# An encoder block with pooling and mLSTM branches: the pooling mixer folded into the input weights, gating and weight splitting moved, row mathematics transposed on TensorE

## The chip, the cores and the metric

The kernel runs on one core of a Trainium2 chip. The metric is the device time in microseconds of one execution, as a median over runs. TensorE (PE in the profile) multiplies matrices, VectorE (DVE), ScalarE (ACT) and GpSimd (POOL) do the rest, and SyncE (SP) issues all DMA transfers from one queue, in order.

## What is computed

The input x is 2048 tokens by 1024 channels in float32. It is normalised and multiplied with one wide matrix, whose columns give u and z (pooling branch), q, k, v, o, z_b and 16 gate columns (mLSTM branch), and the merge gates g_a and g_b.

```python
h = rms_norm(x, norm_pre_g)
u_a, z_a, q, k, v, o, z_b, gates, g_a, g_b = split(h @ w_in)
pooled = multiscale_pool(u_a)              # per group of 256 channels: window mean (2, 4, 8, 16) minus the token
mixed = einsum('bsgc,gcd->bsgd', pooled, pool_mix_w)
y_a = mixed * pool_scale * silu(z_a)
# q, k: depthwise convolution of width 5 and silu; four heads of 256
# two directions of a gated matrix memory in chunks of 128 tokens, with a running maximum over the chunks
y_b = normalised(h_fwd + h_bwd) * sigmoid(o) * silu(z_b)
merged = sigmoid(g_a + b0) * (y_a @ w_proj_pool) + sigmoid(g_b + b1) * (y_b @ w_proj_mlstm)
out = x + rms_norm(merged @ w_out, norm_post_g)
```

Pooling is linear and acts along the tokens, the same for all channels of a group; the mixer is linear and acts along the channels.

## The kernel before

Products are made to about float32 accuracy: each operand is split into a high and a low part (`split`, lines 92 to 99: ScalarE copies the high part, VectorE or GpSimd subtracts the low one), and three matmuls are made for each pair (`mm3`, lines 107 to 109; `acc3`, lines 932 to 934). A few products use plain float32 operands in one matmul, which the profile records as two.

**Phase 1** goes twice over 1024 tokens (a half). `operands` loads the transposed x in two blocks of 512 columns, scales it with the rows `rb` of inverse norms, and makes the eight operand blocks A11 to S4. In the first half `sums(b)` squares each block on ScalarE, adds the squares on VectorE, and adds over the partitions with matmuls into `ssqp` (line 249). Then 36 pairs of 128 columns follow in an order that `in_pairs` writes out; each after the first two is a product of seven blocks by a Strassen-like scheme (`strassen`), 84 matmuls of 512 columns, in PSUM banks A, B and C. The weights of a pair stand in the pool `wc` (20 rooms, 14 to a pair, a high and a low part in each two). In the first half `prep_w` makes them and `keep_w` stores four of seven combinations; in the second half `again_w` loads those and splits the rest. The `pair_...` functions take the results: `pair_qk` convolves, `pair_v` transposes (`vtr`, line 661), `pair_u` pools and stores `pooled`, `pair_z` stores silu(z) as `zs`, `pair_g` and `pair_o` store gates.

In the second half `row_math`, a generator taken one step further at the pairs of `ROWS`, works out the gates' running sums and maxima: 128 rows (direction, head, chunk) of 128 tokens. The ends of the rows go to DRAM (`ends`, line 859) and come back with four heads as rows (line 864) for the scan over the chunks; the result goes out (`carry`) and back as a column. `masked` makes the exponents' masks through the pool `wt` (three rooms) from pair 10 on.

**The tail** begins with `mlstm`, 64 steps (head, chunk). It takes callbacks: at step 32 `aside` loads and splits the mixer's maps and part of `w_proj_pool`, at step 57 `then` more of it, at step 63 `mixer(0)` runs. `mixer(t)` takes 256 tokens: it loads `pooled` and `zs`, splits, multiplies with the maps (`mps`), scales and gates on VectorE, and splits the result into `pys`. `branch_a` multiplies `pys` with `w_proj_pool` (`paps`) for eight token tiles, with `mixer(t + 2)` behind the second column tile. `branch_b` and `output` follow. A scheduler orders each engine's instructions by priority and expected times; `issue_after` ties one behind another.

## Time and profile before

| | us |
|---|---|
| median of 3 runs | 2377.75 (2377.66 to 2380.99) |
| profiled execution | 2386.15 |
| its span, first to last instruction | 2384.3 |
| PE, DVE, ACT, POOL busy | 2314.4, 1466.4, 900.0, 1138.0 |
| mean granted clock of TensorE | 0.991 |

Phase 1 has its first product at 20.7 us and its last at 1470, the mLSTM loop's transposes of k start at 1470.4, the matmuls of branch A at 1793.4; the last of them starts at 2029.6. Branch B and the output follow. Busy time says how long an engine had an instruction in hand. A matmul's duration overlaps with its neighbours', so the pace of matmuls is read from their number in a stretch. Waits are put down to the releaser that came last.

### The profile page before, as it was taken

To read this page: it belongs to the slowest core of one execution; us is meant where nothing else is said; L and a number is where in the kernel's file an instruction comes from. 1 tells how busy PE (TensorE), PEld (TensorE's weight loads), DVE (VectorE), ACT (ScalarE), POOL (GpSimd) and SP (SyncE) were. 2 spreads that over 40 slices of the span, in tenths; PEclk is the share of its full clock that TensorE was granted. 3 is DMA by queue.
4 is the path that set the end of the run, shared out by engine and by line. 5 is a ranking of instruction groups with operands and counts; after the bars stand their busy time and mean duration, and the time that the engine had idled before them with its cause. 6 is when DMAs were issued, how large, how long until landed. Compare 5 with 4: busy or idle time off the path is not lost.

```text
span 2384.3 us, 35775 instructions
## 1 busy us (share of the span) xinstructions
PE 2314.4 (97%) x12569; PEld 2001.0 (84%) x12569; DVE 1466.4 (62%) x2495; ACT 900.0 (38%) x1773; POOL 1138.0 (48%) x902
## 2 busy tenths in 40 slices
PE   6899999999999989999999999999999999999998
PEld 4688888888888878888888887998989899999786
DVE  6876666677666464455666534888975333354765
ACT  4434433333343423222322333776764111121442
POOL 4655565565545334464564540554565111233775
PEclk9999999999999999999999999999999999999999
DMA  4567656566673566878777876777657546588763
GB/s 138 174 215 276 238 207 230 208 208 223 237 259 137 178 185 201 260 262 273 253 254 244 260 250 245 226 217 234 204 159 233 174 148 207 187 279 283 248 215 124
DMA packets 303011, 521.63 MB, mean 219 GB/s; under 512 B 27504, under 2 KB 138224, under 8 KB 302832
## 3 DMA queue, kind: packets, MB, share of 16 engines
q1 hardware_dynamic: 302832, 519.35, 65.1%
q8 instruction: 99, 1.62, 0.3%
q14 instruction: 80, 0.66, 0.1%
HBM read 318.45 MB, written 200.80 MB: 218 GB/s over the span
## 4 chain that ended last, share of the span: by engine, by line
PE 79%; DVE 7%; DMA 6%; issue 3%; POOL 3%; ACT 2%; SPq 1%; POOLq 0%; DVEq 0%; ACTq 0%
PE bankB L107 8%; PE bankB L108 7%; PE bankB L109 7%; PE bankA L109 5%; PE bankA L108 5%; PE bankA L107 5%; PE bankC L108 5%; PE bankC L107 5%; PE bankC L109 5%; PE num L1232 4%; PE pb L933 2%; PE pb L932 2%; PE pb L934 2%; PE paps L933 2%; PE paps L932 2%
## 5 line engine op out<-in xcount | busy, mean ns | idle before, releaser
L99 POOL TENSOR_TENSOR wB21l<-wraw,wB21h 128x512 fp32r<-128x512 f32 x76 | 106.7, 1405 | 228.3 <-ACT wB21h L95 190.7
L635 DVE SCALAR_TENSOR_TENSOR acc<-raw,conv_w,acc 128x1026 f32<-128x1026 f32 (+1 forms) x96 | 153.8, 1615 | 10.6 <-ACT acc L630 9.7
L99 POOL TENSOR_TENSOR wB22l<-wraw,wB22h 128x512 fp32r<-128x512 f32 x76 | 115.6, 1521 | 87.3 <-ACT wB22h L95 55.2
L1216 POOL TENSOR_TENSOR qs<-q,isc 128x256 f32<-128x256 f32 x120 | 91.2, 762 | 134.2 <-PE num L1232 53.0
L933 PE MATMUL pb<-oxs,w_proj_mlstmh 128*128 128x256 f32 x512 | 144.0, 281 | 0.0
L932 PE MATMUL pb<-oxs,w_proj_mlstmh 128*128 128x256 f32 x512 | 143.6, 281 | 0.0
L934 PE MATMUL pb<-oxs,w_proj_mlstml 128*128 128x256 f32 x512 | 143.4, 280 | 0.0
L933 PE MATMUL paps<-pys,w_proj_poolh 128*128 128x256 f32 x512 | 142.9, 281 | 0.2 <-POOL pys L99 0.2
L932 PE MATMUL paps<-pys,w_proj_poolh 128*128 128x256 f32 x512 | 141.4, 281 | 0.0
L934 PE MATMUL paps<-pys,w_proj_pooll 128*128 128x256 f32 x512 | 141.1, 280 | 0.0
L99 POOL TENSOR_TENSOR wB11l<-wraw,wB11h 128x512 fp32r<-128x512 f32 x72 | 106.9, 1485 | 56.0 <-ACT wB11h L95 52.8
L398 DVE TENSOR_TENSOR u<-bankB,p 128x512 f32<-128x512 f32 x76 | 52.2, 687 | 103.0 <-PE bankB L109 95.8
L107 PE MATMUL bankC<-S1h,wT1h 128*128 128x512 f32 x272 | 106.8, 393 | 3.4 <-ACT sg L746 3.4
L107 PE MATMUL bankB<-S3h,wT3h 128*128 128x512 f32 x272 | 106.8, 393 | 2.3 <-DVE u L398 2.3
L109 PE MATMUL bankB<-S2h,wT2l 128*128 128x512 f32 x272 | 106.2, 390 | 1.3 <-DVE wT2l L99 1.3
L107 PE MATMUL bankB<-A22h,wT4h 128*128 128x512 f32 x272 | 106.1, 390 | 1.3 <-DVE u L403 1.3
L108 PE MATMUL bankB<-S2l,wT2h 128*128 128x512 f32 x272 | 106.9, 393 | 0.0
L107 PE MATMUL bankA<-A12h,wB21h 128*128 128x512 f32 x272 | 106.6, 392 | 0.1
L916 POOL TENSOR_TENSOR nm<-nm,mask 128x256 f32<-128x256 f32 x64 | 61.3, 972 | 95.2 <-DMA nm<-negM 84.6
L108 PE MATMUL bankB<-S3l,wT3h 128*128 128x512 f32 x272 | 106.7, 392 | 0.0
L109 PE MATMUL bankB<-S3h,wT3l 128*128 128x512 f32 x272 | 106.6, 392 | 0.0
L108 PE MATMUL bankC<-S1l,wT1h 128*128 128x512 f32 x272 | 106.5, 392 | 0.0
(443 smaller groups left out, 7729.2 us busy)
## 6 DMA issues: line engine op xcount, KB each, us to landing
wraw<-in_w_in SPq DMA_DIRECT2D x110, 512.0 KB, 4.6
wt<-wT2h SPq DMA_DIRECT2D x34, 256.0 KB, 4.7
wt<-wT1h SPq DMA_DIRECT2D x34, 256.0 KB, 4.4
wt<-wT3h SPq DMA_DIRECT2D x34, 256.0 KB, 3.4
wt<-wT2l SPq DMA_DIRECT2D x34, 256.0 KB, 4.8
wt<-wT1l SPq DMA_DIRECT2D x34, 256.0 KB, 4.0
wt<-wT3l SPq DMA_DIRECT2D x34, 256.0 KB, 2.9
wt<-wT4h SPq DMA_DIRECT2D x34, 256.0 KB, 2.0
```

Source lines behind the costliest of these rows:

```text
L99: return eng.tensor_tensor(lo, x, hi.bitcast(F32), op=ALU.subtract)
L107: nc.tensor.matmul(ps, wh, xh, start=start and kt == 0, stop=False, skip_group_check=True)
L108: nc.tensor.matmul(ps, wh, xl, start=False, stop=False, skip_group_check=True)
L109: nc.tensor.matmul(ps, wl, xh, start=False, stop=stop and kt == 3, skip_group_check=True)
L398: self.read_banks.append(nc.vector.tensor_tensor(u2, bank["B"], p1, op=ALU.add))
L635: nc.vector.scalar_tensor_tensor(acc[:, :n], raw[:, tap : tap + n], self.cw[:, ct, tap : tap + 1], acc[:, :n], op0=ALU.mult, op1=ALU.add,)
L916: nc.gpsimd.tensor_tensor(t[:, d, :, :], t[:, d, :, :], mask[:, d, None, :].to_broadcast([P, 2, P]), op=ALU.add)
L932: nc.tensor.matmul(ps, wh, xh, start=i == 0, stop=False)
L933: nc.tensor.matmul(ps, wh, xl, start=False, stop=False)
L934: nc.tensor.matmul(ps, wl, xh, start=False, stop=i == n)
L1216: nc.gpsimd.tensor_tensor(qs[d], q[:, :, ck], isc[:, d, j % 2, None, :].to_broadcast([P, 2, P]), op=ALU.mult)
L1232: nc.tensor.matmul(pn, qs[d][:, kt, :], state[:, kt, :], start=kt == 0, stop=False)
```

## The change

- **Mixer's maps folded into weights.** `fold` multiplies the columns of w_in that make u with the maps, scaled by `pool_scale` (GpSimd), in eight steps of eight plain float32 matmuls in the first half, and stores them as `wu`; the pairs u of both halves load these. The mixer of the tail goes, with its maps.
- **Gating in pair_z.** Each z pair loads `pooled`, multiplies it with silu(z) on GpSimd and stores the result `ya` in place of `zs`; the z pairs come later in the order. In the tail `pooled_load` and `pooled_split` take the place of `mixer`.
- **The pooled projection's weights** are split in the second half (`split_ahead`, pairs 12 to 27, through the pool `wt`), stored as high and low parts (`wp`), and loaded whole in the mLSTM loop, every fourth step, at steps 58 to 61 and behind the loop.
- **Row mathematics.** The ends are turned into rows by matmuls (`re`), scanned on one partition, and turned back by matmuls (`rc`). No transfer is left between.
- **The start.** The norms of the first half's second block come from rows of x, squared and summed on ScalarE (`row_sums`), in place of `sums(1)`. xT is laid out by blocks and loaded two k tiles at a time; in the first half the first weights' low parts are made on VectorE.
- **Layouts.** A weight's high and low parts share a tile (`wc` has 10 rooms of twice the size, `w1`, `w1b` and `w2` likewise) and one DMA; w_in is laid out so that each quarter is contiguous.

The core of the diff:

```diff
-ROWS = (3, 4, 6, 7, 9, 10)
+PRE = 12
+FOLDS = (2, 5, 7, 9, 12, 14, 16, 18)
+ROWS = (3, 4, 6, 7, 9)
 PB = 2
 NB = 3
 W2 = 40
 EARLY = 0
-PX = "kT"
-LASTN = 63
+MORE = 57
+YA = (50, 54, 62)
...
             ps = psum.tile([P, 4], F32, tag="tr", name=self.nm("ssqp"), bufs=2)
             for i in range(4):
                 nc.tensor.matmul(ps[:, i : i + 1], acc[:, i * P : (i + 1) * P], self.one_c, start=True, stop=True)
-            if b == 0:
-                busy(acc[:, :P], acc)
+            busy(X[7][0][:, :P], X[7][0])
             ssq = pool.tile([P, 4], F32, tag="ssq", name=self.nm("ssq"), bufs=2)
-            ends = self.rstd_of(ssq, ps, 0, b)
-            self.rows_of(0, b, rb[:, b * BLK : (b + 1) * BLK], psum)
-            if b == 0:
-                busy(self.rstd[:, :1].to_broadcast([P, P]), acc)
+            ends = self.rstd_of(ssq, ps, 0, 0)
...
+            busy(self.rstd[:, :1].to_broadcast([P, P]), X[7][0])
             return ends
+
+        def row_sums():
+
+            self.rows_read = []
+            part = pool.tile([P, 8], F32, tag="ssq", name=self.nm("part"), bufs=2)
+            tiles = []
+            for k in range(8):
+                xs = (pool.tile if k < 5 else self.wt_pool.tile)([P, BLK], F32, tag="p" if k < 5 else "wt", name=self.nm("xs"))
+                r0 = BLK + k % 4 * P
+                self.rows_read.append(nc.sync.dma_start(xs, a["x"][r0 : r0 + P, k // 4 * BLK : (k // 4 + 1) * BLK]))
+                tiles.append(xs)
+            return part, tiles
 
...
             for kt in range(KT):
-                if half == 0 and b == 0 and kt == 2:
-                    with tc.issue_after(scaled[1].ins):
-                        sums(1)
+                if half == 0 and b == 0 and kt == 6:
+                    with tc.issue_after(scaled[5].ins):
+                        assert not xs
+                        nc.vector.tensor_tensor(part[:, :4], part[:, :4], part[:, 4:], op=ALU.add)
+                        self.known = self.rstd_of(part[:, :4], part[:, :4], 0, 1)[0]
+                        self.rows_of(0, 1, rb[:, BLK:], psum)
...
+                if half == 0 and b == 0 and kt > 0:
+                    with tc.issue_after(self.upper.ins):
+                        for _ in range(min(2, len(xs))):
+                            k = 8 - len(xs)
+                            x = xs.pop(0)
+                            nc.scalar.activation(x, x, AF.Square, accum_out=part[:, k : k + 1])
             self.scaled = scaled
...
+    def columns(self, i):
+        kind, g = self.pairs[i][:2]
+        return self.sp[f"wu{g}"] if kind == "u" else self.a["w_in"][i]
+
+    def fold(self, pool, psum):
+
+
+        nc, a, tc = self.nc, self.a, self.tc
+        for g in range(4):
+            for half in range(2):
+                room = self.rows.tile([P, HALF], F32, tag="rb", name=self.nm("fm"))
+                m, sc = room[:, : 2 * DH].rearrange("p (c n) -> p c n", c=2), room[:, 2 * DH : 3 * DH]
+                nc.sync.dma_start(m, a["pool_mix_w"][g])
+                nc.sync.dma_start(sc, a["pool_scale"][g * DH : (g + 1) * DH].partition_broadcast(P))
+                w = pool.tile([P, 2, 4 * P], F32, tag="acc", name=self.nm("fw"))
+                nc.sync.dma_start(w, a["w_uT"][g, :, :, half * 4 * P : (half + 1) * 4 * P])
+                yield
+                nc.gpsimd.tensor_tensor(m, m, sc[:, None, :].to_broadcast([P, 2, DH]), op=ALU.mult)
+                for k2 in range(2):
+                    ps = psum.tile([P, 2, DH], F32, tag="tr", name=self.nm("fps"), bufs=2)
+                    for k in range(2):
+                        n0 = (k2 * 2 + k) * P
+                        with tc.issue_after(self.third.ins):
+                            for ct in range(2):
+                                nc.tensor.matmul(
+                                    ps[:, k, :], w[:, ct, n0 : n0 + P], m[:, ct, :], start=ct == 0, stop=ct == 1
+                                )
+
+                    o = pool.tile([P, 2, 2, P], F32, tag="p", name=self.nm("fo"))
+                    for e in range(2):
+                        nc.scalar.activation(o[:, e], ps[:, :, e * P : (e + 1) * P], AF.Copy)
+                    nc.sync.dma_start(self.sp[f"wu{g}"][:, half, :, k2 * 2 : k2 * 2 + 2], o)
+                yield
...
-        o = []
+        o, pooled = [], []
+        off, n, tstart = (0, HALF - 8, 0) if half == 0 else (8, HALF + 8, HALF - 8)
 
         def body(i, b, x):
             if not o:
-                o.extend(pool.tile([P, HALF], F32, tag="acc", name=self.nm("zs")) for _ in range(2))
-            d = o[i][:, b * BLK : (b + 1) * BLK]
+                o.extend(pool.tile([P, HALF + 8], F32, tag="acc", name=self.nm("zs")) for _ in range(2))
+            d = o[i][:, off + b * BLK : off + (b + 1) * BLK]
             nc.scalar.activation(d, x, AF.Sigmoid)
             nc.vector.tensor_tensor(d, x, d, op=ALU.mult)
 
-        yield from self.pointwise(H, W, psum, pool, body)
+        for part, _ in enumerate(self.pointwise(H, W, psum, pool, body)):
+            if part == 2:
+                for i in range(2):
+                    pooled.append(pool.tile([P, HALF + 8], F32, tag="acc", name=self.nm("pu")))
+                    nc.sync.dma_start(pooled[i][:, :n], self.sp[f"pooled{g}"][:, i, tstart : tstart + n])
+            yield
         for i in range(2):
-            nc.sync.dma_start(self.sp[f"zs{g}"][:, i, half * HALF : (half + 1) * HALF], o[i])
+            ct = 2 * g + i
+            if half == 0:
+                nc.scalar.activation(self.halo_z[:, ct, :], o[i][:, HALF - 8 : HALF], AF.Copy)
+            else:
+                nc.scalar.activation(o[i][:, 0:8], self.halo_z[:, ct, :], AF.Copy)
+            nc.gpsimd.tensor_tensor(pooled[i][:, :n], pooled[i][:, :n], o[i][:, :n], op=ALU.mult)
+            nc.sync.dma_start(self.sp["ya"][:, ct, tstart : tstart + n], pooled[i][:, :n])
...
-        src = self.sp["ends"].rearrange("q (d h c) -> d h q c", d=2, h=NH)
+
+        ps = psum.tile([1, 2, P], F32, tag="tr", name="re", bufs=2)
+        for k in range(2):
+            nc.tensor.matmul(ps[:, k, :], ends[:, k : k + 1], self.ident, start=True, stop=True)
+        sc, leaves = T(2 * P, 1).rearrange("o (q r) -> o q r", q=2), one[:1, :]
+        nc.scalar.activation(sc, ps, AF.Copy)
+        chunks = lambda x, d: x[:, d * 64 : (d + 1) * 64].rearrange("o (h c) -> o h c", h=NH)
+        for d, at in enumerate((0, NC_ - 1)):
+
+            nc.vector.memset(chunks(sc[:, 0, :], d)[:, :, at : at + 1], NEG)
+            row = slice(d * 64, d * 64 + 64) if d == 0 else slice(127, 63, -1)
+            nc.vector.tensor_tensor_scan(
+                leaves[:, row], sc[:, 0, row], sc[:, 1, row], NEG, op0=ALU.add, op1=ALU.max
+            )
+        enters = sc[:, 0, :]
+        nc.vector.memset(enters, NEG)
         for d in range(2):
-            nc.sync.dma_start(sc[:, d, :, :], src[d])
+            to, of = (slice(1, NC_), slice(0, NC_ - 1)) if d == 0 else (slice(0, NC_ - 1), slice(1, NC_))
+            nc.vector.tensor_copy(chunks(enters, d)[:, :, to], chunks(leaves, d)[:, :, of])
         yield
-        car = T(64, NH).rearrange("h (d q c) -> h d q c", d=2, q=2)
-        nc.vector.memset(car, NEG)
...
-        yield
+        ps = psum.tile([P, 2], F32, tag="tr", name="rc", bufs=2)
+        for k, row in enumerate((enters, leaves)):
+            nc.tensor.matmul(ps[:, k : k + 1], row, self.one_c[:1, :], start=True, stop=True)
         mc = T(2)
-        nc.sync.dma_start(mc, self.sp["carry"].rearrange("q r -> r q"))
...
+    def split_ahead(self, e, kt):
+
+        nc = self.nc
+        x, hi = (self.wt_pool.tile([P, 512], F32, tag="wt", name=self.nm("wp")) for _ in range(2))
+        nc.sync.dma_start(x, self.a["w_proj_pool"][:, kt, e * 512 : (e + 1) * 512])
+        self.split(hi.bitcast(F32R), x.bitcast(F32R), x, "act", "dve")
+        for p, t in enumerate((hi, x)):
+            nc.sync.dma_start(self.sp["wp"][:, kt, e, p], t)
...
+    def pool_weights(self, W, e, kts, pool):
+
+        for kt in kts:
+            t = pool.tile([P, 2, 512], F32R, tag="w", name=self.nm("w_proj_pool"))
+            W[kt, e] = t[:, 0], t[:, 1]
+            self.nc.sync.dma_start(t.bitcast(F32), self.sp["wp"][:, kt, e])
...
-    def mixer(self, t, mix, ya):
-        nc, sp = self.nc, self.sp
-        cut = slice(t * TT, (t + 1) * TT)
+    def pooled_load(self, t, ya):
+        ya[t] = []
+        for u in range(2):
+            ya[t].append(self.pair_of("kT", "xa", F32))
+            self.nc.sync.dma_start(
+                ya[t][u].rearrange("p a b t -> p (a b) t"), self.sp["ya"][:, 4 * u : 4 * u + 4, t * TT : (t + 1) * TT]
+            )
+
+    def pooled_split(self, t, ya):
         for g in range(4):
-            xz = self.pair_of("kT", "xz", F32)
-            nc.sync.dma_start(xz[:, 0], sp[f"pooled{g}"][:, :, cut])
-            nc.sync.dma_start(xz[:, 1], sp[f"zs{g}"][:, :, cut])
-            z = xz[:, 1]
-            xs = self.pair_of(PX, "pxs")
-            self.split(xs[:, 0], xs[:, 1], xz[:, 0], "act", "dve")
             ys = ya[t, g] = self.pair_of("v1h" if g < 2 else "v1l", "pys")
-            for i in range(2):
-                ps = self.psum.tile([P, 512], F32, tag="t", name=self.nm("mps"), bufs=PB)[:, :TT]
-                self.acc3(
-                    ps,
-                    [
-                        (tuple(w[:, kt, i * P : (i + 1) * P] for w in mix[g]), (xs[:, 0, kt, :], xs[:, 1, kt, :]))
-                        for kt in range(2)
-                    ],
-                )
-                ct = 2 * g + i
-                nc.vector.scalar_tensor_tensor(
-                    z[:, i, :], ps, self.pscale[:, ct : ct + 1], z[:, i, :], op0=ALU.mult, op1=ALU.mult
-                )
...
-    def mlstm(self, aside=None, then=None, last=None):
+                    self.pooled_load(t + 2, ya)
+                if d == 4 and t + 2 < n:
+                    self.pooled_split(t + 2, ya)
...
-            w1 = es.enter_context(tc.tile_pool(name="w1", bufs=12, side="right", reuse_waits="tile"))
-            raws = es.enter_context(tc.tile_pool(name="wraws", bufs=4, side="right", reuse_waits="tile"))
+            w1 = es.enter_context(tc.tile_pool(name="w1", bufs=8, side="right", reuse_waits="tile"))
             self.kv = es.enter_context(tc.tile_pool(name="kv", bufs=KV, reuse_waits="tile"))
...
-
-            def aside():
-                mix.extend(self.mix_weights(raws, w1))
-                WA.update(self.weights("w_proj_pool", 0, range(2), raws, w1))
-
-            def then():
-                held.append(es.enter_context(tc.tile_pool(name="w1b", bufs=8, side="right", reuse_waits="tile")))
-                WA.update(self.weights("w_proj_pool", 0, range(2, 6), raws, held[0]))
-
-            held = []
-            self.mlstm(aside, then, lambda: self.mixer(0, mix, ya))
+            WA, ya, held = {}, {}, []
+
+            def more():
+                if not held:
+                    held.append(es.enter_context(tc.tile_pool(name="w1b", bufs=4, side="right", reuse_waits="tile")))
+                self.pool_weights(WA, 1, [len(WA) - KT], held[0])
+
+            turns = {4 + 4 * kt: lambda kt=kt: self.pool_weights(WA, 0, [kt], w1) for kt in range(KT)}
+            turns |= {MORE + 1 + k: more for k in range(4)}
+            turns |= {YA[t]: lambda t=t: self.pooled_load(t, ya) for t in range(2)}
+            turns[YA[2]] = lambda: self.pooled_split(0, ya)
+            self.mlstm(turns)
             w1b = held[0]
             self.xp = es.enter_context(tc.tile_pool(name="xp", bufs=2, reuse_waits="tile"))
-            w2 = es.enter_context(tc.tile_pool(name="w2", bufs=36, side="right", reuse_waits="tile"))
-            self.mixer(1, mix, ya)
-            WA.update(self.weights("w_proj_pool", 0, range(6, 8), raws, w2))
-            WA.update(self.weights("w_proj_pool", 1, range(8), raws, w2))
-            self.branch_a(WA, mix, ya)
+            raws = es.enter_context(tc.tile_pool(name="wraws", bufs=4, side="right", reuse_waits="tile"))
+            w2 = es.enter_context(tc.tile_pool(name="w2", bufs=16, side="right", reuse_waits="tile"))
```

## Rows read from the trace of the kernel before

**Rows 1.** The page, part 1: busy us (share of the span), instructions.

```profile
PE 2314.4 (97%) x12569; PEld 2001.0 (84%) x12569; DVE 1466.4 (62%) x2495; ACT 900.0 (38%) x1773; POOL 1138.0 (48%) x902
```

**Rows 2.** Busy time by stretch: us, each engine's busy us (instructions), clock, DMA share, GB/s.

```profile
1200.00:1320.00 120.00, 119.53 (x536) 98.81 (x535) 74.64 (x94) 32.20 (x49) 63.36 (x44) 1.00 0.76 253
1440.00:1800.00 360.00, 345.79 (x2294) 318.25 (x2293) 285.73 (x928) 237.93 (x676) 163.66 (x206) 0.99 0.67 212
2040.00:2160.00 120.00, 120.00 (x1018) 120.00 (x1017) 57.93 (x98) 19.91 (x32) 36.45 (x43) 1.00 0.74 253
```

**Rows 3.** Waits of PE, whole span: who waited for whom, total us, times, longest.

```profile
PE ssqp L249 <- DVE sq L245: 15.5, 2, 12.3
PE vtr L661 <- DVE vnl L99: 7.2, 1, 7.2
PE mps L932 <- ACT pxs L95: 6.3, 5, 2.3
...
PE num L1232 <- ACT h L1265: 3.6, 3, 1.9
...
PE s L1205 <- DVE gb L1286: 3.3, 1, 3.3
...
PE bankA L431 <- DVE A11l L99: 1.9, 1, 1.9
PE s L1205 <- ACT kn L1145: 1.5, 1, 1.5
```

**Rows 4.** Waits of PE from 130 to 700 us: the only one.

```profile
PE vtr L661 <- DVE raw L602: 0.2, 1, 0.2
```

**Rows 5.** Busy time by stretch, behind four waits; the clock stands third from the end.

```profile
40.30:47.10 6.80, 6.80 (x20) 5.63 (x20) 0.16 (x1) 0.00 (x0) 1.02 (x1) 0.50 0.01 2
...
862.90:869.70 6.80, 3.24 (x12) 2.95 (x13) 4.20 (x14) 1.68 (x3) 0.00 (x0) 0.50 0.86 275
...
1644.50:1651.30 6.80, 6.17 (x29) 6.18 (x30) 3.55 (x11) 5.16 (x16) 2.73 (x3) 0.50 0.99 289
...
1764.00:1767.40 3.40, 3.39 (x10) 2.83 (x11) 1.51 (x8) 1.89 (x6) 1.44 (x3) 0.50 0.72 261
```

**Rows 6.** Groups of PE by form: line, tiles, shapes, count, busy us, mean ns, idle before.

```profile
L932 PE MATMUL mps<-pxs,mxh 128*128 128x256 f32 x128 | 35.6, 290 | 7.8 <-ACT pxs L95 6.3 <-DVE gb L1286 1.1 <-DVE xz L1036 0.3
```

**Rows 7.** Timeline of PE in the mLSTM loop: start us, us, instruction, count.

```profile
1501.76 1.04 PE L1232 MATMUL num<-cb,qs 128*128 128x258 f32 x4
...
1502.75 0.28 PE L1236 MATMUL num<-v,sd 128*128 128x258 f32 x1
```

**Rows 8.** Timeline of SP's DMA issues around the row mathematics.

```profile
847.47 0.37 SPq L859 DMA_DIRECT2D ends<-rows  x1
...
857.23 0.31 SPq L864 DMA_DIRECT2D rows<-ends  x1
```

**Rows 9.** Busy time by stretch, between these two issues.

```profile
850.00:855.00 5.00, 4.86 (x26) 3.89 (x25) 1.84 (x3) 1.72 (x3) 3.20 (x3) 1.00 0.83 45
```

**Rows 10.** Timeline of DVE in the same place; in brackets the idle time before.

```profile
862.73 0.07 DVE L655 MEMSET vnl<- 128x8 f32 x1 [10.18 <-DMA qT<-acc]
```

**Rows 11.** Timeline of ACT in the mLSTM loop.

```profile
1639.40 1.14 ACT L95 ACTIVATE mxh<-mraw 128x512 fp32r<-128x512 f32 x2
```

**Rows 12.** Timeline of DVE at the start.

```profile
5.32 0.69 DVE L245 TENSOR_TENSOR sq<-sq,sq 128x512 f32<-128x512 f32 x1 [3.69 <-ACT sq L243]
...
50.26 7.47 DVE L197 SCALAR_TENSOR_TENSOR xT<-xT,norm_pre_g,rb 128x512 f32<-128x512 f32 x8 [8.43 <-ACT rb L185]
...
70.99 1.78 DVE L206 TENSOR_TENSOR xT<-xT,xT 128x512 f32<-128x512 f32 x1
```

**Rows 13.** Groups of POOL by form.

```profile
L766 POOL TENSOR_TENSOR gB<-gB,gB 128x1024 f32<-128x1024 f32 x16 | 41.4, 2589 | 15.4 <-DVE gB L763 14.1 <-PE bankC L108 1.3
```

**Rows 14.** Groups of DVE by form.

```profile
L398 DVE TENSOR_TENSOR u<-bankB,p 128x512 f32<-128x512 f32 x76 | 52.2, 687 | 103.0 <-PE bankB L109 95.8 <-ACT p L392 5.7 <-ACT raw L639 1.2
```

**Rows 15.** Waits of SP's queue from 720 to 1440 us.

```profile
SPq L919 <- DMA nm<-negM: 15.8, 9, 4.7
```

205 lines of the change are left out of this document (104 added, 101 removed).

## The prediction

> **What bounds the kernel now.** I read the page first, for the busy shares: the matrix engine is busy for 97% of the span [rows 1]. A busy share alone doesn't show that the engine runs at its pace, so I then read the busy time by stage and divided it by the instructions. In a quiet stretch of the projections 119.53 us hold 536 matmuls of 512 columns, 223 ns each; in the last projection 120 us hold 1018 of 256 columns, 118 ns each [rows 2]. The reader should see that the pace follows the columns and that nothing else shows in it. So TensorE sets the time, and two things count: matmuls taken off or put on, each at its pace, and stretches in which TensorE stands still or runs slowly.
>
> For the second I read who waited for whom on TensorE. The list is short: a second wait for the sums of squares at the start (15.5 us in two waits of which the longest, 12.3, is the start itself; 3.2 remain), one of 7.2 before a transpose of v, 6.3 in the mixer, and small ones in the mLSTM loop [rows 3]. Over 570 us of the first half it waits 0.2 us in all [rows 4]. Last I read the clock in the stretches behind the longer waits: it is granted at 0.50, the lower of its two levels (1.2 against 2.4 GHz), for 6.8 us behind the wait at the start, for 6.8 behind the transposes, for 6.8 and for 3.4 in the mLSTM loop [rows 5]. Such a stretch costs half its length again: 3.4, 3.4, 3.4 and 1.7 us.
>
> **The mixer leaves the tail.** Eight token tiles x four groups x two column tiles x six matmuls = 384 matmuls of 256 columns go; their row shows 128 for each of three lines [rows 6]. At the pace of 118 ns that is -45.3 us, all on the path, since TensorE has no slack there. The mean of 290 ns in that row overlaps with the neighbours and isn't the price. The 6.3 us that mixer matmuls waited for ScalarE's split go too: the gated columns now come ready from memory and are split for a tile two tiles later: -6.3.
>
> **The fold comes into the first half.** Eight steps of eight matmuls, 64 in plain fp32 with 256 columns. The nearest row is the mLSTM numerator with fp32 operands and 258 columns: two of them (four records) and one cheap matmul run from 1501.76 to 1502.75 [rows 7]; (0.99 - 0.12) / 2 = 0.435 us each, x 256/258 = 0.43. 64 x 0.43 = +27.6 us, again fully on the path. From below it could be 64 x 0.118 = 7.6 if plain fp32 ran at the split pace, but the row is the same kind of instruction, so I take 27.6. Each step's operands are fetched a pair (84 x 223 ns = 18.7 us) ahead, and its ScalarE copies and GpSimd scaling are a few microseconds per step; I cost them at nothing, covered by that pair. If the cover fails, a step waits for its two scratch banks.
>
> **Row mathematics.** Before, 256 single floats go to memory at 847.47 and come back from 857.23 on [rows 8]. In between the transfers nearly stop: 45 GB/s while the DMA engines count as 83% busy [rows 9]. VectorE's next memset waits 10.2 us for the landing of an earlier store of q [rows 10], the split of v is queued behind that, and TensorE waits for it. With the ends transposed on TensorE neither trip remains: -7.2 - 3.4 = -10.6. The four new matmuls have at most 128 columns; with the fp32 price as an upper end they are under 1.7 us, and I take +1. They stand two pairs behind the VectorE steps that feed them, so I cost no wait; below, nothing excludes a small one.
>
> **Weights in the mLSTM loop.** The loop's waits at 1638 and 1643 (3.3 and 1.5 us) [rows 3] come when ScalarE and VectorE split the mixer's and the pooled projection's weights between the loop's own steps: the splits stand in ScalarE's row there [rows 11]. The change leaves only loads at these places: -3.3 - 1.5 - 3.4 (clock) = -8.2. The later batch goes likewise: of the waits for ScalarE's h one of 1.9, and 1.7 of clock: -3.6. The stage's whole idle time bounds this: 360 - 345.8 = 14.2 us [rows 2]. What was split there is split in the second half instead: 16 steps of one ScalarE copy, one VectorE subtraction, one load and two stores. VectorE is busy 75 of 120 us and ScalarE 32 there [rows 2], so the arithmetic hides.
>
> **The start.** The second block's squares no longer pass through VectorE adds and matmuls, but through eight loads of x and ScalarE's accumulator. The second wait for the sums (3.2), its slow stretch (3.4) and the wait for A11l behind those adds (1.9) may go: 8.5. Against it stand 2 MB more to fetch ahead of the second block, and rb of the second block, whose arrival set VectorE's scaling at 50.26 [rows 12]; TensorE will want it some 8 us sooner. Ends: 0 and -8.5; I take -6, since VectorE, not the transfers, was the late engine.
>
> **Pooled gating.** Sixteen GpSimd products of about 128x1024 at 2.6 us [rows 13], 16 loads and some halo copies join the z pairs; the two stores keep their number. GpSimd is busy 63 of 120 us in the second half [rows 2]; the same product already ends every o pair without a TensorE wait [rows 4]. Zero, covered by the three weight rooms (10 less the 7 of a pair) that TensorE has ahead, 3 x 12 x 223 ns = 8.0 us. If GpSimd ran later than that, the low parts of the next weights would be late.
>
> The row of a VectorE addition with both operands in SBUF shows 0.69 us with GpSimd idle, and of a subtraction 1.78 with it busy [rows 12]. The Trainium skill (SBUF — State Buffer, Who interferes with whom) says why: such an instruction and a GpSimd one that reads SBUF take turns on one port, each for its whole length. By that rule 16 products could hold VectorE for 16 x 2.6 = 42 us. The trace agrees on the single instruction, but the additions that empty the banks have one operand in PSUM and keep 687 ns [rows 14], so by the trace the sum stays.
>
> **Transfers.** The second half moves about 253 GB/s at a share of 0.76 [rows 2]. The new splits bring 4.2 MB in and 8.4 MB out over 300 us, 42 GB/s more: share 0.76 x 295/253 = 0.89, an estimate. They also take two of the three rooms of the wt pool, which the mask steps use; SP already waits there for a mask load, nine times, 4.7 us at most [rows 15], and the weight loads are queued behind it. Ends: 0, and 16 x 4.7 = 75 less the lead; near the low end, since a single hold is shorter than the lead of 8.0. For all new waits together +3.
>
> **Sum.** -45.3 - 6.3 + 27.6 - 10.6 + 1 - 8.2 - 3.6 - 6 + 3 = -48.4 us. The profiled execution took 2386.15 (span 2384.3): 2337.8 by its own clock. The median of the runs, 2377.75, is 8.4 below; I take the same difference off it: **2329 us**.
>
> **Rivals.**
> 1. *Only the counted matmuls move.* The waits come back elsewhere, since another engine's work was only shifted: -45.3 + 27.6 + 1 + 3 = -13.7, 2364 us. For it speaks that the split work is only moved to the second half. Against it, each wait above has its cause by name and loses it. 0.11.
> 2. *The mLSTM loop runs freer still.* Of its 14.2 us of idle time [rows 2] I counted waits of 3.3 + 1.5 + 1.9 = 6.7; ScalarE and VectorE, relieved of the splits, may return the other 7.5 as well. With the whole 8.5 at the start and no new wait that is 7.5 + 2.5 + 3 = 13 further: 2316 us or below. For it speaks that VectorE is the next busiest engine there (286 of 360 us); against it, that the small waits aren't all its. 0.18.
> 3. *Slower: SP is held in the second half.* Place: pairs 12 to 27, where the split steps and the masks pass three rooms. Price: what one hold exceeds the lead of 8.0 us by, and half of a slow stretch behind it. It decides from 53/16 = 3.3 us of TensorE standing or slow per step (53 is the gain with the 0.2% on top); at 5 us per step it is 2329 + 80 = 2409. The longest hold of 4.7 us speaks against it. 0.05.
> 4. *The port.* The GpSimd products hold VectorE and so the banks: 2329 + 42 = 2371, if each holds TensorE for its whole length. The Trainium skill's rule named above would be behind it. The 16 products of the o pairs, of which half fall into the first half with its 0.2 us of waits [rows 4], speak against. 0.04.
> 5. *No change.* Folds and late loads eat the rest, within 0.2%: 0.03.
>
> The forecast, 2317 to 2342, has 0.59. The range is 2308 to 2356: it takes in the start's ends, rival 2 and part of rival 1. Within 0.2% (4.8 us), about what a measurement can tell from no change, lies 0.03; slower gets 0.06 (rival 3, and 0.01 for a port that costs more than its price); faster 0.91 (the forecast, rivals 1 and 2, and 0.03 of rival 4).
>
> **What would show it.** Right: no matmul of the mixer in the tail and the pooled projection at 118 ns without ScalarE waits; 128 fold records at about 215 ns pace before 450 us; no wait near the second half's row mathematics and the clock at 1.00 there; no wait for ScalarE or VectorE in the mLSTM loop above 1 us where the weights were split; the first long product pair begun without a second wait for squares. Wrong: TensorE waits in pairs 12 to 27 of the second half with SP held by the wt pool; waits in the first half at the fold; a wait at the fifth column tile of the first token tile, whose weights now arrive whole from memory; VectorE draining banks late next to the z pairs.

## The result, and the profile after

The changed kernel takes **2353.91 us** (median; 2349.06 to 2356.05), the kernel before 2379.37 beside it on the same chip: ratio 0.9892 [0.9876, 0.9907], 25.5 us less. Measured again on a later chip the ratio was 0.9881 [0.9865, 0.9897]. Its profiled execution took 2356.05, span 2354.3. The direction was forecast rightly. The time lies inside 2308 to 2356, 2.1 us under the upper end, but outside the forecast's 2317 to 2342, and 24.9 us above the 2329 at its centre: half of the expected gain isn't there. Of these, 6.3 are the profiled executions: the one of before lay 8.4 us above the median of its runs (2377.75), that of after only 2.1. The rest, some 18 us, is in the trace.

The page, part 1, against [rows 1]: 256 instructions fewer on TensorE, the 384 mixer matmuls less 128 records of fold matmuls (64 in plain fp32, two records each).

```profile
PE 2296.3 (98%) x12313; PEld 1978.7 (84%) x12313; DVE 1414.7 (60%) x2417; ACT 886.3 (38%) x1795; POOL 1177.0 (50%) x900
```

To see where the time came from, both spans are cut at the first matmul of four stages in TensorE's timeline: the second half's gates (748.8 us before, 767.5 after), the mLSTM loop (1470.4, 1492.3), the second projection of the output stage, `pb` (2029.8, 1997.7), and the end. The forecast's terms fall into these pieces:

| piece | before | after | forecast | measured | terms |
|---|---|---|---|---|---|
| start and first half | 748.8 | 767.5 | +21.6 | +18.7 | start -6, fold +27.6 |
| second half | 721.6 | 724.8 | -6.6 | +3.2 | row mathematics -10.6 +1, new waits +3 |
| mLSTM loop and pooled projection | 559.4 | 505.4 | -63.4 | -54.0 | mixer -45.3 -6.3, loop -8.2 -3.6 |
| the rest | 354.5 | 356.6 | 0 | +2.1 | |
| span | 2384.3 | 2354.3 | -48.4 | -30.0 | |

Nearly all that is missing lies in two pieces: the second half came out 9.8 short of its forecast, and the loop and projection 9.4. The kernel of experiment 4, which differs from the one before in the row mathematics alone, takes 746.8, 558.9 and 356.1 us for the first, third and last piece, so pieces repeat within some 2 us.

Waits of TensorE after, to be held against [rows 3]: the second wait for the sums of squares is down to 0.6 us, the mixer's and the one before `vnl` are gone, and new ones stand in the list.

```profile
PE bankB L109 <- DVE u L468: 5.8, 3, 3.2
PE fps L372 <- ACT gsb L670: 5.6, 1, 5.6
PE num L1325 <- ACT h L1358: 4.8, 4, 2.7
PE vtr L743 <- DVE raw L684: 4.5, 2, 4.1
...
PE paps L1037 <- DMA w_proj_pool<-wp: 1.8, 1, 1.8
...
PE paps L1038 <- POOL pys L101: 1.0, 1, 1.0
```

Busy time by stretch, columns as in [rows 2]: the row mathematics' place, then three stretches at the lower clock, then 20 us of the pooled projection around the loop's last matmuls.

```profile
845.00:870.00 25.00, 23.98 (x106) 19.52 (x106) 22.60 (x39) 7.78 (x10) 9.91 (x5) 1.00 0.46 157
...
1228.20:1235.00 6.80, 5.91 (x18) 4.95 (x19) 3.35 (x6) 1.20 (x2) 2.18 (x3) 0.50 0.92 268
1750.50:1753.90 3.40, 3.31 (x9) 2.83 (x10) 2.84 (x12) 3.40 (x11) 3.40 (x5) 0.50 0.11 43
1835.80:1842.60 6.80, 5.64 (x26) 5.64 (x27) 0.53 (x1) 0.00 (x0) 1.65 (x1) 0.50 1.02 371
...
1820.00:1830.00 10.00, 9.18 (x78) 8.98 (x77) 3.15 (x7) 3.21 (x8) 2.29 (x2) 1.00 0.02 7
1830.00:1840.00 10.00, 7.16 (x45) 6.56 (x44) 3.46 (x3) 3.35 (x6) 4.71 (x3) 0.79 0.99 325
```

The reader should see that the place of the row mathematics is now quiet: full clock, and the 45 GB/s at a share of 0.83 of [rows 9] are gone. The slow stretch of 6.8 us that stood there ([rows 5], 862.9) has a successor at 1228.2. The loop's at 1644.5 is gone and the one at 1764 has a successor at 1750.5. A new one stands at 1835.8, behind ten microseconds in which the transfers fell to 7 GB/s and ten in which they ran at 325 with TensorE waiting.

What stands behind `vtr` and the banks in the second half is read on VectorE's side. The waits of VectorE from 980 to 1330 us, two of its rows:

```profile
DVE wp L101 <- ACT wp L97: 44.9, 14, 7.9
...
DVE vnh L736 <- DMA kT<-acc: 4.3, 2, 3.5
```

ScalarE's own rows in the same stretch:

```profile
ACT wp L97 <- DMA wp<-in_w_proj_pool: 26.5, 7, 8.1
ACT wp L97 <- DMA nm<-nm: 20.2, 5, 7.1
```

VectorE's subtraction for a late split (`wp`) waits for ScalarE's copy, and that copy waits for the load or for a room of `wt` from which a mask (`nm`) is still being stored. Both engines work in order, so a bank's reading behind it stands too. That gave the first theory for the second half; the experiments had to show whether these 44.9 us are the price.

### The profile page after: what moved, and what is told of

It reads as the page before. It is cut to its first block, busy times and chain, and to the rows that moved or that the text cites. A ratio compares the mean times of both kernels' runs of the same rounds, so it can differ in the third digit from the quotient of the medians.

```text
span 2354.3 us, 34514 instructions
## 1 busy us (share of the span) xinstructions
PE 2296.3 (98%) x12313; PEld 1978.7 (84%) x12313; DVE 1414.7 (60%) x2417; ACT 886.3 (38%) x1795; POOL 1177.0 (50%) x900
## 5 line engine op out<-in xcount | busy, mean ns | idle before, releaser
L101 POOL TENSOR_TENSOR wB<-wraw,wB 128x512 fp32r<-128x512 f32 x224 | 339.6, 1520 | 287.9 <-ACT wB L97 213.1
L97 ACT ACTIVATE wB<-wraw 128x512 fp32r<-128x512 f32 x228 | 141.9, 626 | 290.3 <-PE bankB L111 133.3
L101 POOL TENSOR_TENSOR wT<-wt,wT 128x512 fp32r<-128x512 f32 x102 | 148.4, 1457 | 134.3 <-ACT wT L97 107.3
L1037 PE MATMUL paps<-pys,w_proj_pool 128*128 128x256 f32 x512 | 145.4, 284 | 2.7 <-DMA w_proj_pool<-wp 1.8
L1038 PE MATMUL paps<-pys,w_proj_pool 128*128 128x256 f32 x512 | 145.1, 284 | 1.0 <-POOL pys L101 1.0
L1039 PE MATMUL paps<-pys,w_proj_pool 128*128 128x256 f32 x512 | 144.6, 283 | 0.0
L1038 PE MATMUL pb<-oxs,w_proj_mlstm 128*128 128x256 f32 x512 | 143.7, 281 | 0.0
L1037 PE MATMUL pb<-oxs,w_proj_mlstm 128*128 128x256 f32 x512 | 143.7, 281 | 0.0
L1039 PE MATMUL pb<-oxs,w_proj_mlstm 128*128 128x256 f32 x512 | 143.5, 280 | 0.0
L109 PE MATMUL bankB<-A22h,wT 128*128 128x512 f32 x272 | 106.5, 392 | 2.6 <-DVE u L473 2.6
L109 PE MATMUL bankA<-A12h,wB 128*128 128x512 f32 x272 | 108.6, 399 | 0.0
L109 PE MATMUL bankC<-S4h,wB 128*128 128x512 f32 x272 | 106.4, 391 | 1.0 <-DVE raw L684 1.0
L110 PE MATMUL bankA<-A12l,wB 128*128 128x512 f32 x272 | 106.7, 392 | 0.0
L111 PE MATMUL bankA<-A12h,wB 128*128 128x512 f32 x272 | 106.7, 392 | 0.0
L111 PE MATMUL bankB<-A22h,wT 128*128 128x512 f32 x272 | 106.5, 392 | 0.0
L110 PE MATMUL bankB<-S2l,wT 128*128 128x512 f32 x272 | 106.5, 392 | 0.0
```

What stands on the lines that cost most here:

```text
L97: self.upper = nc.scalar.activation(hi, x, AF.Copy)
L101: return eng.tensor_tensor(lo, x, hi.bitcast(F32), op=ALU.subtract)
L109: nc.tensor.matmul(ps, wh, xh, start=start and kt == 0, stop=False, skip_group_check=True)
L110: nc.tensor.matmul(ps, wh, xl, start=False, stop=False, skip_group_check=True)
L111: end = nc.tensor.matmul(ps, wl, xh, start=False, stop=stop and kt == 3, skip_group_check=True)
L1037: nc.tensor.matmul(ps, wh, xh, start=i == 0, stop=False)
```

## The experiments

Each kernel is compared by its ratio to the kernel before, run beside it, and by its stages. The second half, from its first long product (60 us behind its gates) to the loop, holds identical code in the changed kernel (665.0 and 666.1), and in the kernels without fold, with a later fold and with weights taken early (665.2, 667.8, 668.3): mean 666.5, within 2 us. In the kernel before it is 661.7. The loop and pooled projection, where nothing is edited there, go from 500.6 to 506.0.

**1. No splits in the second half.** One split instead of 16; the later loads all read that one block, so the pooled projection is computed with wrong weights.

```diff
-                    if half == 1 and PRE <= i < PRE + 2 * KT:
+                    if half == 1 and i == PRE:
...
-            self.nc.sync.dma_start(t.bitcast(F32), self.sp["wp"][:, kt, e])
+            self.nc.sync.dma_start(t.bitcast(F32), self.sp["wp"][:, 0, 0])
```

> The changed kernel with one of the sixteen weight splits of the second half left in; the tail loads that one result sixteen times, so the output is not the reference's. Theory: the second half's new waits (4.1 us before a transpose of v, two of 1 to 3 us for bank drains, with a slow stretch of 6.8 us) come from the splits' ScalarE, VectorE and transfer work, so the second half (first product bankC<-S1h to the first transpose of k) falls from 665.0 to about 653 us and the time from 2353.9 to about 2342. Rival: they come from the new order of the pairs (v behind k) and GpSimd products on VectorE's port; then the second half stays within 3 us of 665 and the time within 4 us of 2353.9.

Measured: 2344.89 us, ratio 0.9836 [0.9812, 0.9861]. The second half takes 656.8, 9.7 less than 666.5, and TensorE's waits in it shrink. Its longest there, from 830 us to the loop:

```profile
PE vtr L743 <- DVE raw L684: 2.3, 2, 1.2
```

The stretch itself in the changed kernel, then here:

```profile
827.40:1492.30 664.90, 656.07 (x2910) 540.89 (x2909) 373.74 (x476) 206.44 (x318) 329.46 (x211) 0.99 0.77 262
827.40:1484.30 656.90, 652.61 (x2911) 538.92 (x2910) 364.61 (x461) 198.71 (x303) 331.37 (x211) 1.00 0.73 248
```

The stretch less TensorE's busy time is its idle time: 8.8 us there, 4.3 here. The rest of the difference is mostly the slow stretch at 1228.2, which is missing here. So the splits do cost what the row mathematics freed, and nearly all of it is TensorE's waits and the lower clock behind them, above all at the pair that transposes v (4.1 us of waiting there, 1.2 here). The new order of the pairs and the gating are in this kernel too; its 656.8 lies near the 655.2 of experiment 4, which has neither.

**2. No fold.** The eight fold steps are left out and the u pairs read the unfolded weights, so the mixer's maps are missing from the output.

```diff
-        return self.sp[f"wu{g}"] if kind == "u" else self.a["w_in"][i]
+        return self.a["w_in"][i]
...
-                    next(fold)
```

> The changed kernel without the fold: the u pairs load the unfolded columns, so mixing and scaling are left out of the output. Theory: the 64 plain fp32 matmuls cost 0.43 us each, 27.6 us, and the waits and slow stretches at the first fold step (5.9 + 3.4) go too: 2353.9 - 37 = 2317, and another 3.6 if the wait at 228 us is the fold's. Rival: a fold matmul costs no more than a split one (0.118 us), and the first half grew by something else: 2353.9 - 7.6 - 9.3 = 2337.

Measured: 2321.14 us, ratio 0.9742 [0.9722, 0.9762], span 2318.4. The second half's gates come at 736.5 instead of 767.5: the fold costs 31.0 us there, against the +27.6 of the sum. The other kernels with the same fold reach that point at 764.2 to 768.2, so 27.7 to 31.7 fits as well. The rival's 2337 falls. Some 5 us more are missing later, where nothing was edited.

**3. The first fold step later.** It stood ahead of the first long pairs, where its second batch waits. TensorE's timeline there:

```profile
80.55 1.89 PE L372 MATMUL fps<-fm,fw 128*128 128x256 f32 x8
88.04 3.73 PE L372 MATMUL fps<-fm,fw 128*128 128x256 f32 x8 [5.61 <-ACT gsb L670]
```

The first eight records are four matmuls. They follow each other at (1.89 - 0.38) / 7 = 0.216 us, since a single record takes 0.38: 0.43 for a matmul at full clock, the price worked out from [rows 7]. The second four run in a slow stretch (84.8 to 91.6 us, clock 0.50), after 5.6 us in which a scratch bank still holds the gates' result.

```diff
-FOLDS = (2, 5, 7, 9, 12, 14, 16, 18)
+FOLDS = (3, 5, 7, 9, 12, 14, 16, 18)
...
-                if half == 0:
-                    next(fold)
```

> The changed kernel with the first fold step at pair 3 instead of pair 2 and its loads behind pair 2. Theory: the first step waits for a scratch bank that the gates' result still holds, because ScalarE empties it only behind the second pair's weights; one pair later the bank is free, so the wait of 5.6 us and its slow stretch of 6.8 us go: 2353.9 - 9 = 2345, and no wait of fps for ScalarE above 1 us. Rival: TensorE then meets the same late ScalarE and VectorE at the next bank drains, as the kernel before did at 87 to 104 us (7 us and two slow stretches of 3.4): within 3 us of 2353.9.

Measured: 2354.86 us, ratio 0.9885 [0.9858, 0.9911], no gain. The time to the first `bankC<-S1h` product falls by 9.2 us and the first half behind it grows by 10.3 (the step's own eight matmuls move from the one to the other). The fold wait goes and others take its place, the longest:

```profile
PE bankA L109 <- ACT p L462: 2.0, 1, 2.0
PE bankB L109 <- DVE u L473: 1.8, 1, 1.8
PE bankA L499 <- ACT A11h L97: 1.4, 1, 1.4
PE bankB L109 <- DVE u L468: 1.3, 1, 1.3
PE bankA L109 <- ACT sg L838: 1.3, 1, 1.3
```

Up to the second half's gates TensorE is idle for 21.0 us in all, against 20.8 in the changed kernel: ScalarE and VectorE are late at that point anyway, and the fold stood in time that TensorE would have waited.

**4. The row mathematics alone**, put into the kernel before.

```diff
-        nc.sync.dma_start(self.sp["ends"].rearrange("q r -> r q"), ends)
+            nc.tensor.matmul(ps[:, k, :], ends[:, k : k + 1], self.ident, start=True, stop=True)
```

> The kernel before with the new row mathematics alone. Theory: the wait of 7.2 us and its slow stretch (3.4) were the small transfers' doing and go, the four matmuls cost 1 us at most: 2379.4 - 10 = 2369.5, with no wait of vtr. Rival: v's transposes wait there anyway, because VectorE's row mathematics stands in front of the drains: within 3 us of 2379.

Measured: 2378.54 us, ratio 0.9979 [0.9965, 0.9993], 5 us less than the kernel before. The wait of 7.2 us is gone (`vtr` waits 0.9 in all from 830 us to the loop), and the second half falls from 661.7 to 655.2: -6.5 where -9.6 was forecast. In the kernel before, the slow stretch begins inside the wait:

```profile
862.90:866.50 3.60, 0.04 (x1) 0.04 (x1) 2.47 (x8) 0.00 (x0) 0.00 (x0) 0.50 0.97 321
866.50:869.70 3.20, 3.20 (x12) 2.91 (x13) 1.73 (x7) 1.68 (x3) 0.00 (x0) 0.50 0.73 224
```

TensorE was busy in 3.2 of its 6.8 us only, so the lower clock cost 1.6 on top of the wait and not 3.4.

**5. Late weights of the pooled projection not loaded.** The last four blocks of the second column tile reuse the tiles of the first four, so that projection is computed with wrong weights.

```diff
-            self.pool_weights(WA, 1, range(4, 8), w2)
+            WA.update({(kt, 1): WA[kt - 4, 1] for kt in range(4, 8)})
```

> The changed kernel without the last four weight loads behind the mLSTM loop: the second half's k tiles 4 to 7 are multiplied with the weights of 0 to 3, so the output is not the reference's. Theory: the wait of 1.8 us for these loads and the slow stretch of 6.8 us behind it are branch A's loss: the stretch from the first paps to the first pb falls from 200.6 to about 195 us, the time by 5 us. Rival: the wait for pys just ahead of it (1.0 us) brings the slow stretch as well, and less than 3 us comes back.

Measured: 2351.76 us, ratio 0.9861 [0.9843, 0.9879]. From the first `paps` matmul to the first `pb` it takes 193.3 instead of 200.6 (196.4 to 200.6 in the eight other traces in which nothing else is changed there, so some 5 us, as the theory has it). The time falls by 2.1 us by the medians and by 5 to 7 by the ratios. The same two stretches as above:

```profile
1820.00:1830.00 10.00, 10.00 (x87) 10.00 (x86) 2.89 (x12) 4.78 (x11) 3.30 (x3) 1.00 0.17 58
1830.00:1840.00 10.00, 10.00 (x87) 10.00 (x86) 5.15 (x7) 2.53 (x4) 3.52 (x4) 1.00 0.75 251
```

The only wait of TensorE that is left from 1780 to 2000 us:

```profile
PE num L1325 <- ACT h L1358: 1.1, 1, 1.1
```

In the changed kernel these four loads stand in SP's queue behind the loop's last store (`yb`, line 1425), for which the queue stood 14.9 us, and are issued together. SP's wait, then the loads in its timeline:

```profile
SPq L1425 <- DVE sga L1152: 14.9, 1, 14.9
```

```profile
1829.90 3.02 SPq L1058 DMA_DIRECT2D w_proj_pool<-wp  x4
```

**6. No pooled gating.** The pooled columns aren't loaded and not multiplied; the gates alone are stored.

```diff
-            nc.gpsimd.tensor_tensor(pooled[i][:, :n], pooled[i][:, :n], o[i][:, :n], op=ALU.mult)
-            nc.sync.dma_start(self.sp["ya"][:, ct, tstart : tstart + n], pooled[i][:, :n])
+            nc.sync.dma_start(self.sp["ya"][:, ct, tstart : tstart + n], o[i][:, :n])
```

> The changed kernel with the z pairs storing silu(z) alone: no load of pooled and no GpSimd product, so the gating is left out of the output. Theory (as predicted): the products and loads cost nothing, the time stays within 4 us of 2354 (ratio 0.989 to the kernel before). Rival: the products hold VectorE and the loads the transfers; then both halves shrink and the time falls by 8 us or more (ratio under 0.986).

Measured: 2351.62 us, ratio 0.9861 [0.9839, 0.9884], an interval that overlaps with the changed kernel's; the second half takes 662.1. By the medians 2 us come back, by the ratios 5 to 7, with some 14 at the far end of the intervals. That lies between the theory and the rival and decides for neither; the 42 us of the fourth rival it excludes.

**7. The transfers of the splits alone.** One split is computed; the other 15 steps load and store unsplit blocks, so the projection's weights are wrong. These 15 steps also take one room of `wt` instead of two.

```diff
-        x, hi = (self.wt_pool.tile([P, 512], F32, tag="wt", name=self.nm("wp")) for _ in range(2))
+        x, hi = (self.wt_pool.tile([P, 512], F32, tag="wt", name=self.nm("wp")) if k or kt == e == 0 else None for k in (1, 0))
...
-        self.split(hi.bitcast(F32R), x.bitcast(F32R), x, "act", "dve")
-        for p, t in enumerate((hi, x)):
+        if kt == e == 0:
+            self.split(hi.bitcast(F32R), x.bitcast(F32R), x, "act", "dve")
+        for p, t in enumerate((hi, x) if kt == e == 0 else (x, x)):
```

> The changed kernel with all loads and stores of the sixteen weight splits in the second half and the arithmetic of one only: the loaded columns are stored twice, and the tail loads the one split result, so the output is not the reference's. Theory A: the second half's loss comes from VectorE, which stands 45 us in all behind ScalarE's copy, which stands behind the load; without both the second half falls from 665.0 to about 657 us, as without the splits (656.8). Theory B: it comes from the transfers (300 GB/s, share 0.88) and the three rooms; then the second half stays above 662.

Measured: 2347.52 us, ratio 0.9847 [0.9827, 0.9867], second half 659.2. Of the 9.7 us, 2.4 come with the transfers, little more than the spread of 2 us, and 7.3 with the two instructions and the second room of each step, which this edit doesn't tell apart.

**8. The loads a pair ahead**, into another pool.

```diff
+                    if half == 1 and PRE <= i + 1 < PRE + 2 * KT:
+                        with tc.issue_after(self.read.ins):
+                            self.load_ahead(*divmod(i + 1 - PRE, KT), pool)
```

> The changed kernel with each split's load issued a pair earlier, into a room of the pool p; everything else and the result as before. Theory A: ScalarE and VectorE then find the columns there, VectorE's wait of 45 us for the splits falls under 15 and the second half from 665.0 to about 658 us; the time falls by about 7 us (ratio about 0.986). Theory B (transfers): no gain, second half above 662.

Measured: 2354.5 us, ratio 0.9875 [0.9849, 0.9901], second half 662.5. The edit didn't do what it was for: the splits were scheduled right behind the earlier loads, and the two engines went on standing for them, VectorE even longer than the 44.9 us of the changed kernel. From 980 to 1400 us:

```profile
DVE wp L101 <- ACT wp L97: 65.8, 14, 14.5
```

So it doesn't decide between the two theories. But with 21 us more of VectorE standing, the second half isn't longer; it is 4 us under the mean.

**9. The splits held back.** Loads a pair ahead as in 8, and the splits tied behind the first reading of a bank in their pair.

```diff
+                    if half == 1 and PRE <= i < PRE + 2 * KT:
+                        with tc.issue_after(self.read_banks[0].ins):
+                            self.split_ahead(*divmod(i - PRE, KT))
```

> The 14 splits of the pooled projection's weights in the second half are tied behind the first read of a product bank of their pair, and their load is issued one pair earlier, so that neither ScalarE's copy nor VectorE's subtraction should stand for a transfer. Theory (the loss in the second half is the two in-order engines standing for a load): VectorE's wait for wp falls from 19 us to under 5, the second half from 665 to 657 to 660 us as in the kernel that has no split, the ratio to the kernel before by 0.002 to 0.003 lower than that of the changed kernel on the same chip. Rival (it is the 14 splits' own work, 14 times 1.2 us on each of the two engines, ahead of the bank reads): the waits for wp go and the second half stays within 2 us of 665.

Measured: 2349.34 us, ratio 0.9864 [0.9846, 0.9882], second half 663.4. VectorE no longer waits for `wp`. Still the second half gains only 3 us, and its `vtr` wait stays, 2.9 us long instead of 4.1. ScalarE's row among the waits from 980 to 1330 us, and then VectorE's for the memset:

```profile
ACT wp L97 <- DMA wp<-in_w_proj_pool: 50.8, 12, 5.9
```

```profile
DVE vnh L739 <- DMA kT<-acc: 6.4, 1, 6.4
```

ScalarE goes on standing for the loads; VectorE, no longer held by `wp`, stands at `vnh`'s memset until an earlier store of k has landed, as it did for a store of q in [rows 10]. The kernel without splits (1) has that wait too, just as long, and TensorE waits only 1.2 us behind it:

```profile
1219.48 0.07 DVE L736 MEMSET vnh<- 128x8 f32 x1 [6.42 <-DMA kT<-acc]
```

So the memset alone isn't the price either.

**10. Three edits together**: 9; the first splits of the pooled columns (`pys`) in the loop tied to the step they are meant for; the pooled projection's first two blocks in half groups that alternate.

```diff
-                    with tc.issue_after(cur["load"].ins):
+                    with tc.issue_after(cur["load"].ins if n != YA[2] else self.step.ins):
...
-        for t in range(n):
+        parts = [(0, 0), (1, 0), (0, 4), (1, 4)] + [(t, d) for t in range(2, n) for d in (0, 4)]
+        for t, d0 in parts:
```

> As the kernel of later splits, and two edits more: the first split of the pooled weights in the last mLSTM steps is tied to a ScalarE instruction of the step that it was meant for, and the first two blocks of the last stage are computed in half groups that alternate, so that the late halves of the weights are wanted later. Theory: the ScalarE wait of 3.6 us at 1745 goes with the 2.7 us wait of the numerator behind it and the 3.4 us of half clock (mLSTM 304.7 to about 301); the half clock of 6.8 us at 1836 goes (the stage from first paps to first pb 200.6 to about 194 us); all three together about 12 to 16 us under the changed kernel. Rival: the waits only move to the next late transfer, and it is within 5 us of the kernel of later splits.

Measured: 2342.76 us, ratio 0.9832 [0.9816, 0.9848]; the changed kernel beside it 2353.77:

> The changed kernel itself on the same chip as the two above, for comparison: ratio to the kernel before 0.989 as before, within 0.002.

So it is 11.0 us faster than the changed kernel. Loop and pooled projection together take 495.4 instead of 503.6 to 505.4. The single stages moved otherwise than expected: the loop grew to 310.2 and the projection's stage fell to 185.2, since 67 of the loop's matmuls that ran behind the first `paps` now run ahead of it; only their sum can be compared. The slow stretches of the loop and of the projection are gone: the clock is 1.00 from 1440 to 1860 us. On the same chip edit 9 alone is 4.4 us faster than the changed kernel, so the two further edits bring 6.6; how much each of them brings wasn't separated. The same stretches as in 5:

```profile
1820.00:1830.00 10.00, 9.44 (x81) 9.23 (x79) 4.65 (x8) 2.60 (x5) 1.19 (x1) 1.00 0.72 215
1830.00:1840.00 10.00, 9.45 (x78) 9.26 (x79) 2.86 (x6) 1.74 (x4) 2.29 (x3) 1.00 0.94 359
```

**11. The late splits on VectorE alone**, on top of 10.

```diff
-        self.split(hi.bitcast(F32R), x.bitcast(F32R), x, "act", "dve")
+        self.split(hi.bitcast(F32R), x.bitcast(F32R), x, "dve", "dve")
```

> As the kernel of all three edits, and the 14 late splits of the second half wholly on VectorE (both parts, behind the bank read), so that ScalarE, which went on standing some 50 us for the loads of wp there when only VectorE's subtraction was tied, no longer has any of this work. Theory (an in-order engine that stands for a load delays what the products wait for): the second half falls from 664 to 657 to 660 us and the time by 4 to 7 us under the kernel of all three edits. Rival (VectorE's own work is what is late there): 14 more VectorE operations of about 0.65 us lengthen the second half by 0 to 5 us.

Measured: 2346.03 us, ratio 0.9835 [0.982, 0.9849], the same as 10. The second half takes 667.5, so the theory falls: with ScalarE rid of the loads nothing is gained. The rival's 0 to 5 us fit (3.7 over the 663.8 of 10), though the spread is nearly as large. VectorE's and TensorE's timelines at the pair that transposes v:

```profile
1228.47 0.07 DVE L739 MEMSET vnh<- 128x8 f32 x1 [11.80 <-DMA kT<-acc]
1228.53 0.69 DVE L468 TENSOR_TENSOR u<-bankB,p 128x512 f32<-128x512 f32 x1
```

```profile
1229.28 0.79 PE L109 MATMUL bankB<-S3h,wT 128*128 128x512 f32 x1 [3.85 <-DVE u L468]
```

The memset wants a room that a store of k is still reading; VectorE stands 11.8 us for it, the reading of the bank behind it is late, and TensorE waits 3.9 us. The wait isn't for a split any more. Whether the splits' transfers make that store so late wasn't tested.

## Why the prediction was right in direction and too large

**Counted matmuls: right.** The mixer's 384 matmuls are gone from the tail. The loop and the pooled projection, before and after:

```profile
1470.40:2029.80 559.40, 537.91 (x4018) 513.71 (x4017) 369.82 (x1094) 288.83 (x760) 219.07 (x248) 0.99 0.65 206
1492.30:1997.70 505.40, 491.63 (x3634) 467.86 (x3633) 319.05 (x999) 257.05 (x709) 193.00 (x227) 0.99 0.66 218
```

TensorE's idle time is 21.5 us in the one and 13.8 in the other, and half of its busy time at the lower clock 4.8 and 4.5. What is left, the matmuls' own time, falls by 46.0 us, where 45.3 were forecast. Worked out so for the whole span, the matmuls' own time falls by 14.1 us against the sum's 16.7 (-45.3 + 27.6 + 1), and the waits with their clock fall by 15.9 against 31.7 (all other terms): the miss is in the waits. The fold cost 31.0 us where it was put, against 27.6 from the numerator's row; the matmul itself has the forecast 0.43. That its operands and engines hide at no cost held nearly: the one wait of 5.6 at the first step replaces others (3), and from 130 to 700 us TensorE waits 1.8 in all against the 0.2 of [rows 4].

**Start: right in kind.** Of the second wait for the sums (3.2) 0.6 us are left; the first long product waits 0.7 (for A11h) instead of 1.9. With the fold taken as +27.6 to +31.0, the first piece's +18.7 leaves -9 to -12 for the start, more than the -6; the two misses offset each other in part.

**Row mathematics: the mechanism right, the size off.** Alone it gives -6.5, not -9.6 (4). The wait and its slow stretch went, but the prediction's rule that a slow stretch costs half its length again counts the part inside the wait twice. [rows 5] shows it: TensorE is busy in 3.24 of these 6.8 us. With 1.6 in place of 3.4 the term is -7.2 - 1.6 + 1 = -7.8.

**The failed step: "so the arithmetic hides".** It was argued from shares of busy time, 75 of 120 us on VectorE and 32 on ScalarE. The 16 late splits cost 9.7 us of the second half (1), some 2.4 with their transfers and 7.3 with their instructions and second rooms (7), where +3 was put for all new waits. With the -6.5 of the row mathematics that makes the +3.2 of the table. So a share of busy time wasn't slack here: TensorE waits 2.9 to 4.5 us near the transposes of v in every kernel with these splits, against 1.2 without them, and runs slowly behind it. Which mechanism makes it wait is not shown. The standing for the loads, argued at first, isn't the price by itself: VectorE stands 45 to 66 us for `wp` in kernels whose second half takes 662 to 668 us, and not at all in 9 and 11, which take 663.4 and 667.5. In the changed kernel the reading that TensorE waits for there stood last for nothing that the profile shows:

```profile
1228.35 0.68 DVE L684 TENSOR_TENSOR raw<-bankC,u 128x512 f32<-128x512 f32 x1 [1.75 <-issue]
```

How the 7.3 us divide between standing, the instructions' own time, the rooms and the store of k stays open.

**The second failed step: the waits in the loop and the mixer.** Mixer -6.3, loop -8.2 and -3.6 were taken as lost for good. The piece fell by 54.0; less the 45.3 of the matmuls, 8.7 of these 18.1 came. The numerator's waits for `h` (1.9 of them counted as lost) even grew, from 3.6 to 4.8. The loop's wait at 1643 and its slow stretch went, but `pys`, split in the loop too, was issued ahead of its step, and ScalarE stood for it:

```profile
1748.63 1.15 ACT L97 ACTIVATE pys<-xa 128x512 fp32r<-128x512 f32 x2 [3.61 <-DMA xa<-ya]
```

The numerator waited 2.7 us behind that, with 3.4 us of slow clock. At the end of the loop the weights came in one burst, with waits of 1.8 and 1.0 and 6.8 us of slow clock (3.4 in the second trace of the same kernel). The prediction named a wait where weights now arrive whole from memory as a sign of its being wrong, but gave it no price. Edits 5 and 10 took 6 to 10 us of this piece back.

**Rivals.** Rival 1 came nearest: waits came back elsewhere. By it every freed wait is lost (-13.7 in all), by the forecast none (-48.4); the span's -30.0 lies about midway. That the time fell inside the stated range at all is due to the range taking in part of this rival. Rival 2 found nothing: TensorE's idle time in the loop fell only from 13.2 to 10.1. Rival 3, with 3.3 us per step needed, measured 9.7/16 = 0.6. Rival 4 wanted 42 us; without the gating the kernel is 2 to 7 us faster (6). The additions that empty the banks have one operand in PSUM and kept 684 ns after the change, against 687 in [rows 14]. The Trainium skill's rule behind this rival (SBUF — State Buffer, Who interferes with whom) is for VectorE instructions with two inputs in SBUF; one with at most one, it says, doesn't contend with GpSimd, and the trace agrees. The group of these additions from 980 to 1495 us:

```profile
L468 DVE TENSOR_TENSOR u<-bankB,p 128x512 f32<-128x512 f32 x26 | 17.8, 684 | 38.1 <-PE bankB L111 24.2 <-ACT p L462 8.4 <-issue 4.1
```

## What to carry to other kernels

Matmuls taken off a saturated TensorE or put on it were priced within a few microseconds here; waits taken away were not, since the next late engine or transfer stood close behind, and about half of what was freed came back. A slow stretch costs half of the time in which TensorE is busy in it, so don't count again what lies inside the wait. Work moved onto engines that are half idle still cost 9.7 us, and how long the engines stood for it (0 to 66 us) didn't tell the price: take the work out and see which wait of TensorE's goes. A load queued behind a store that isn't ready is late even where bandwidth is free: look for a stretch of few GB/s followed by one at full share, and see what the queue stood for. Wanting such loads later and tying the early splits to their step brought 6.6 us in edit 10, beyond what edit 9 had brought.

## What the runs showed of the hardware

With a wait on TensorE of only 1.0 to 5.6 us there often went 3.4 or 6.8 us at a granted clock of 0.50, the lower level, also inside the saturated stretches (at 1228.2, 0.9 us before the end of a wait of 4.1; at 1750.5, at the end of one of 2.7). It doesn't follow every such wait: 1.6 us at 1327.9 had none. Half of what lies behind the wait comes on top of it: with 2.7 us waited, 1.7 more.

VectorE instructions with all operands in SBUF took longer beside GpSimd work. Conv steps of one shape in the changed kernel's timeline of VectorE: the first began while GpSimd was idle, the next two began behind a GpSimd addition of 2.85 us (from 1214.99), which a subtraction of 2.27 followed:

```profile
1211.21 1.28 DVE L717 SCALAR_TENSOR_TENSOR acc<-raw,conv_w,acc 128x1026 f32<-128x1026 f32 x1
...
1215.51 5.65 DVE L717 SCALAR_TENSOR_TENSOR acc<-raw,conv_w,acc 128x1026 f32<-128x1026 f32 x2
```

Two of these take 5.65 us instead of 2.6, just ahead of the bank's reading for which TensorE then waited 0.95 us at 1221.
